# Column sums on TensorE in groups: the feature sums of ten layer norms in fours, the modulation sums in pairs

## The chip, the core and the metric

The kernel runs on one core of a Trainium2 chip. The metric is the device time of one execution in microseconds, lower is better. The core has five engines that work side by side, each through a queue of its own in order: TensorE (PE, matrix products; its weight loads are shown apart as PEld), VectorE (DVE), ScalarE (ACT), GpSimd (POOL) and SyncE (SP), which issues the DMA transfers here. They wait for each other through semaphores.

## The reference, cut to what matters

Two layers of a transformer over 1024 latent tokens and 256 context tokens, 1024 features wide. What the change touches is the layer norm and the modulation vectors:

```python
def layer_norm(x, g, b):
    mu = jnp.mean(xf, axis=-1, keepdims=True)
    var = jnp.mean(jnp.square(xf - mu), axis=-1, keepdims=True)
    return (xf - mu) * lax.rsqrt(var + LN_EPS) * g + b
...
for l in range(DEPTH):
    mod = silu_c @ w_ada[l] + b_ada[l]
    mod_c = silu_cc @ w_ada[l] + b_ada[l]
    sh1, sc1, g1, sh2, sc2, g2 = jnp.split(mod, 6, axis=-1)
    o, oc = token_mixers(modulate(x, sh1, sc1), modulate(xc, sh1c, sc1c), ...)
    x = layer_norm(ALPHA * x + g1 * (o @ w_out[l]), ln1_g[l], ln1_b[l])
    x = layer_norm(ALPHA * x + g2 * swiglu(modulate(x, sh2, sc2), ...), ln2_g[l], ln2_b[l])
```

In the first layer the context tokens take the same two residual steps and norms; in the last one they do not.

## The kernel before, in words

Everything is kept with the features on the partitions: a tensor of 1024 features is eight tiles of 128 partitions, with the tokens along the free axis (512, 512 and 256 of them). A dense product is done by `mm3` (L262): each f32 operand is split into a high and a low part (`wunit`, L234, does it for the weights: a DMA into `wraw`, an ACT cast `whi` on L249, a POOL or DVE subtraction `wlo` on L252), and three matmuls per feature tile, all on line L277, are summed in PSUM. `products_g` (L325) runs over the token groups, and an `evac` function takes each result out of PSUM. For the residual steps that is `ev_res` (L1172), which adds the gated product to the residual tile `z` with one DVE instruction (L1176).

A layer norm over features is a sum over partitions, and that is done by TensorE: `fsum` (L353) multiplies each of the eight feature tiles by a 128x32 block of ones. Tile `kt` goes to the column quarter `kt % 4` of the array, so to 32 of the 128 PSUM partitions, and the second four add to the first. The copy `fssb` (L360) takes the four partial sums out, and the next matmul (`mean` L377, or `var` L394) adds them over the quarters. `layer_norm` (L372) calls `fsum` twice: for `z` itself, and for the squares of `z` minus its mean, which ACT makes one by one into 512-wide buffers (`lnsq`, L388). Those buffers come from a pool of five (`t512`, L76) that the copies `fssb`, `meansb`, `rstdsb` and the modulation's `ut` share. After the variance come the reciprocal root on DVE (L343 to L349), `rstd` (L398), and the multiplication, the modulation and the affine step, feature tile by feature tile, on DVE, POOL and ACT. There are ten layer norms, eight over 512 tokens and two over 256. Each is put beside the dense products of the next token group; the last one, at the end of the kernel, has nothing beside it.

The modulation vectors of later stages are made in small steps between dense products. `ada_step` (L172) multiplies and adds one 128x512 block of `w_ada` into two accumulators on DVE (L177, L179), one for the latent and one for the context vector; after eight blocks each accumulator is summed over its partitions by one matmul against 32 columns of ones (L185, into `adaps`), on the quarter `2 * i + s_`. `ada_end` (L140) follows when both halves of a part are there. The first vectors (L138) are made in another way, which the change leaves alone.

The order of instructions in each engine's queue is made by a list scheduler, which simulates the times of the instructions and places each when it finds its inputs ready, earlier lines of the program first. The author steers it with edges: `gate(ins, after)` (L434) asks that `ins` is placed after `after`, with no semaphore, and `in_order` (L440) chains a list of instructions with such edges. `hook` (L297) ties the five steps of the 512-wide first layer norm of a layer to points in the dense matmuls that follow: the matmul that begins at column 6 x 512 of them is placed after the last sum of `z`, the one at 53 x 512 after the last sum of squares (L42).

Of the kernel before, what the change touches and what calls it, by code (L numbers as in the profile page):

```python
# [12 lines left out]
AF = mybir.ActivationFunctionType  # L13
ALU = mybir.AluOpType
# [8 lines left out]
KT = 8  # L23
# [30 lines left out]
def body(ctx: ExitStack, tc, xT, cT, w_ada, w_in, nbias, wa2, w_out, w_fi, w_fo, vecs, cc, consts, ropes, gmask, out):  # L54
    nc = tc.nc
    act, dve, pool, pe = nc.scalar, nc.vector, nc.gpsimd, nc.tensor
# [19 lines left out]
    def t512(name="t5"):  # L76
        return tmp.tile([P, 512], F32, tag="t5", name=name)
# [4 lines left out]
    def bank_x(name):  # L82
        return ps_x.tile([P, 512], F32, tag="x", name=name)

    def bank_a(name):
        return ps_a.tile([P, 512], F32, tag="a", name=name)
# [20 lines left out]
    ones = const.tile([P, 32], F32, name="ones")  # L107
# [10 lines left out]
    scc = const.tile([P, KT, 32], F32, name="scc")  # L118
# [21 lines left out]
    def ada_end(l, streams, ps, sel):  # L140
        sb = t512("adasb")
        act.copy(sb, ps)
        pv = bank_x("adav")
        for m in range(4):
            pe.matmul(pv[:, 4 * m:4 * m + 4], lhsT=sb[:, m * P:(m + 1) * P], rhs=sel, start=True, stop=True)
        for i, (part, half) in enumerate(streams):
            c0 = V_BADA + part * KT + half * 4
            dve.tensor_tensor(
                out=mod[l][:, part, half * 4:half * 4 + 4, :],
                in0=pv[:, 0:16].rearrange("p (m s) -> p m s", s=4)[:, :, 2 * i:2 * i + 2],  # L150
                in1=vec[l][:, c0:c0 + 4].unsqueeze(2).to_broadcast([P, 4, 2]), op=ALU.add)
# [13 lines left out]
    ada_todo, ada_run, ada_st = [], [], {}  # L165
# [6 lines left out]
    def ada_step(l, st, i, k, raw):  # L172
        if k == 0:
            ada_st["acc"] = [spool.tile([P, 512], F32, tag="hl", name="adacc") for _ in range(2)]
        for s_, a in enumerate(ada_st["acc"]):
            if k == 0:
                dve.tensor_scalar(a, raw, scc[:, k, s_:s_ + 1], None, ALU.mult)  # L177
            else:
                dve.scalar_tensor_tensor(out=a, in0=raw, scalar=scc[:, k, s_:s_ + 1], in1=a, op0=ALU.mult, op1=ALU.add)  # L179
        if k == KT - 1:  # L180
            if i == 0:
                ada_st["ps"] = bank_a("adaps")
            for s_, a in enumerate(ada_st["acc"]):
                q = 2 * i + s_
                pe.matmul(ada_st["ps"][32 * q:32 * q + 32, :], lhsT=ones[:, 0:32], rhs=a, start=True, stop=True)  # L185
            if i == 1:
                ada_end(l, st, ada_st["ps"], ident[:, 0:P:32])

# [108 lines left out]
    def hook(products_, offs):  # L297
        hk["c"] = 0
        hooks[:] = zip(offs, products_)
# [38 lines left out]
    def rsqrt_cols(src, n, eps, rows=P):  # L338
        v = small.tile([P, 20], F32, tag="rq_v", name="rq_v", bufs=2)
        y = small.tile([P, 20], F32, tag="rq_y", name="rq_y", bufs=2)  # L340
        t = small.tile([P, 20], F32, tag="rq_t", name="rq_t", bufs=2)
        v, y, t = v[:rows, :n], y[:rows, :n], t[:rows, :n]
        dve.tensor_scalar(v, src, eps, None, ALU.add)  # L343

        dve.tensor_scalar(y.bitcast(I32), v.bitcast(I32), -0.5, 1597463007.0, ALU.mult, ALU.add)
        for _ in range(3):
            dve.tensor_tensor(out=t, in0=y, in1=y, op=ALU.mult)
            dve.scalar_tensor_tensor(out=t, in0=t, scalar=-0.5, in1=v, op0=ALU.mult, op1=ALU.mult)
            dve.scalar_tensor_tensor(out=y, in0=t, scalar=1.5, in1=y, op0=ALU.add, op1=ALU.mult)  # L349
        return y  # L350


    def fsum(src, n):  # L353

        ps = bank_x("fs")
        for kt in range(KT):
            q = kt % 4
            ins = pe.matmul(ps[32 * q:32 * q + 32, :n], lhsT=ones[:, 0:32], rhs=src(kt), start=(kt < 4), stop=(kt >= 4))  # L358
        sb = t512("fssb")
        act.copy(sb[:, :n], ps[:, :n])  # L360
        return sb, ins
# [6 lines left out]

    NPOOL = 4
    NP3 = 3  # L370

    def layer_norm(z, t0, n, eps, consume, npool=NPOOL, offs=None):  # L372
        sl = slice(t0, t0 + n)
        nb = n // P
        sb, x1 = fsum(lambda kt: z[kt][:, sl], n)
        mps = bank_x("mean")
        x2 = pe.matmul(mps[:, :n], lhsT=onesm, rhs=sb[:, :n], start=True, stop=True)  # L377
        msb = t512("meansb")
        act.copy(msb[:, :n], mps[:, :n])
        for kt in range(KT):  # L380
            if kt >= KT - npool:
                pool.tensor_tensor(out=z[kt][:, sl], in0=z[kt][:, sl], in1=msb[:, :n], op=ALU.subtract)
            else:
                dve.tensor_tensor(out=z[kt][:, sl], in0=z[kt][:, sl], in1=mps[:, :n], op=ALU.subtract)

        def sq(kt):
            q = t512("lnsq")
            act.activation(q[:, :n], z[kt][:, sl], AF.Square)  # L388
            return q[:, :n]

        sb, x3 = fsum(sq, n)
        vps = bank_x("var")
        for b in range(nb):
            x4 = pe.matmul(vps[:, b:b + 1], lhsT=sb[:, b * P:(b + 1) * P], rhs=ones1, start=True, stop=True)  # L394
        y = rsqrt_cols(vps[:, :nb], nb, eps)
        rps = bank_x("rstd")
        for b in range(nb):
            x5 = pe.matmul(rps[:, b * P:(b + 1) * P], lhsT=y[:, b:b + 1].to_broadcast([P, P]), rhs=ident,  # L398
                           start=True, stop=True)
        if offs and n == 512:  # L400
            hook((x1, x2, x3, x4, x5), offs)
        rsb = t512("rstdsb")
        act.copy(rsb[:, :n], rps[:, :n])
        for kt in range(KT):
            if kt >= KT - npool:
                pool.tensor_tensor(out=z[kt][:, sl], in0=z[kt][:, sl], in1=rsb[:, :n], op=ALU.mult)
            else:
                dve.tensor_tensor(out=z[kt][:, sl], in0=z[kt][:, sl], in1=rps[:, :n], op=ALU.mult)
            consume(kt, sl)
# [24 lines left out]
    def gate(ins, after):  # L434

        if after is not None:
            tc.add_manual_dep(ins.ins, after.ins.name, NOSYNC, reason="buffers in order of use")
        return ins

    def in_order(inss):  # L440

        for a, b in zip(inss, inss[1:]):
            gate(b, a)
        return inss[-1]
# [80 lines left out]
    for l in range(NL):  # L525
# [35 lines left out]
        for e in range(2):  # L561
            ba = V[:, V_BA + e:V_BA + e + 1]
            for (t0, n) in FULL:
                ps = bank_q("zps")
# [4 lines left out]
        ins = [act.activation(a, a, AF.Exp, scale=-1.0) for a in dec][-1]  # L569
        ins = [gate(act.activation(a, a, AF.Ln, bias=one1), ins) for a in dec][-1]  # L570
# [24 lines left out]
        for p, ga, gb in abanks:  # L595
            dst, src, n = a_mm(p, ga, gb, gk, gq)
# [6 lines left out]
        for lev in range(6):  # L603
# [8 lines left out]
            for p, ga, gb in abanks:  # L612
                dst, src, n = a_mm(p, ga, gb, xk_, X)
# [87 lines left out]
        for p in range(2):  # L701
# [5 lines left out]
            for par in range(2):  # L707
                for g0, g1 in ((0, 8), (8, 10)):
                    pt = bank_q("inc")
                    for g in range(g0, g1):  # L710
                        for e in range(2):
                            for hh in range(2):
                                h, r0 = 2 * p + hh, 64 * e + 32 * hh
                                pe.matmul(pt[r0:r0 + 32, (g - g0) * 64:(g - g0 + 1) * 64],
                                          lhsT=kdt[e][64 * par:64 * par + 64, g * P + 32 * h:g * P + 32 * h + 32],
                                          rhs=vg(g)[64 * par:64 * par + 64, h * 64:(h + 1) * 64], start=True, stop=True)
# [13 lines left out]
            for i in range(1, NCH - 1):  # L730
                for e in range(2):
                    c, nx = order[e][i], order[e][i + 1]
# [3 lines left out]
                                             op0=ALU.mult, op1=ALU.add)  # L736
# [377 lines left out]
        sb = {"n": 0, "t": ps_s.tile([P, 2, 2, 512], F32, tag="s4", name="sT", bufs=1)}  # L1114
# [11 lines left out]
        for x, i in enumerate(PAIRS):  # L1126
            if x < 5:
                load(PAIRS[x + 1])
            if x in (0, 2):
# [3 lines left out]
            a, na, places, skip = (  # L1133
                (some(PAIRS[1], None), steps_a[3], 22, 2), (), (some(PAIRS[3], None), steps_a[3] - half, 22, 2), (),
                (some(PAIRS[5], None), steps_a[3] - half, 22, 2), (iter(()), 0, 39, 0))[x] or (
                chain(some(PAIRS[x + 2], half), some(PAIRS[x + 1], None)), half + steps_a[0], 39, 3)
            live, tails = tails, []
            b = stage_b(i)
            n = done = 0
# [22 lines left out]
        z = []  # L1162
# [9 lines left out]
        def ev_res(g, m):  # L1172
            def ev(ps, t0, n, c):
                s = 0 if t0 < SEQ else 1
                zz = z[m + c][:, t0:t0 + n]
                dve.scalar_tensor_tensor(out=zz, in0=ps[:, :n], scalar=g[:, m + c, s:s + 1], in1=zz,  # L1176
                                         op0=ALU.mult, op1=ALU.add)
            return ev

        groups = GROUPS[l]  # L1180
# [7 lines left out]
        for grp in groups:  # L1188
            for m in range(0 if grp[0][0] >= SEQ else 2, KT):
                dense(w_out[l, :, m * P:(m + 1) * P], oh_all, ol_all, grp, ev_res(ga1, m))  # L1190
            for (t0, n) in grp:
                def consume(kt, sl, t0=t0, n=n):
                    modulate(u2h, u2l, z[kt][:, sl], kt, l, 1, t0, n, dve)
                    affine(AFF1, z[kt][:, sl], aGB[:, 0, kt:kt + 1], aGB[:, 1, kt:kt + 1])
# [51 lines left out]
        for grp in GROUPS[l]:  # L1246
# [4 lines left out]
            for (t0, n) in grp:  # L1251
                def consume2(kt, sl, t0=t0, n=n):
# [6 lines left out]
                    elif t0 < SEQ:  # L1259
                        nc.sync.dma_start(xs[kt * P:(kt + 1) * P, sl], z[kt][:, sl])  # L1260
                layer_norm(z, t0, n, LN_EPS, consume2, NP3 if last else NPOOL)

# [99 lines left out]
```

## Time and profile before

| | us |
|---|---|
| median of three runs | 3704.74 (3701.15 to 3706.63) |
| the profiled execution | 3701.86 |
| its span in the profile | 3700.1 |
| mean granted clock of TensorE | 0.955 of full |

The profile is of one execution. Rows of groups read: line, engine, operation, out<-in, shape (rows*columns of the array that a matmul uses, then the size), x count, busy time in us, mean ns of one, idle time of the engine before them and who ended it. Rows of the timeline read: start in us from the span's start, length, engine, line, operation, count of merged records, and in brackets the idle time before with the one that ended it. Rows of the stretches view give a window, its length, the busy time of the engines, the granted clock, the share of the DMA engines in use and GB/s. An f32 matmul is run in two passes and leaves two records, so the 160 sum matmuls of the layer norms are 320 records on line 358:

```profile
L358 PE MATMUL fs<-z,ones x160: 379/592/636, 929.9 to 3673.1; 128*32 128x512 f32 x128, 128*32 128x256 f32 x32
L358 PE MATMUL fs<-lnsq,ones x160: 379/592/1062, 981.3 to 3683.0; 128*32 128x512 f32 x128, 128*32 128x256 f32 x32
```

A "visit" below is a run of consecutive matmuls of one such sum line in PE's order, between matmuls of other lines.

### The profile page before, as it was taken

To read this page: it belongs to the slowest core of one execution; us is meant where nothing else is said; L and a number is where in the kernel's file an instruction comes from. 1 tells how busy PE (TensorE), PEld (TensorE's weight loads), DVE (VectorE), ACT (ScalarE), POOL (GpSimd) and SP (SyncE) were. 2 spreads that over 40 slices of the span, in tenths; PEclk is the share of its full clock that TensorE was granted. 3 is DMA by queue.
4 is the path that set the end of the run, shared out by engine and by line. 5 is a ranking of instruction groups with operands and counts; after the bars stand their busy time and mean duration, and the time that the engine had idled before them with its cause. 6 is when DMAs were issued, how large, how long until landed. Compare 5 with 4: busy or idle time off the path is not lost.

```text
span 3700.1 us, 49312 instructions
## 1 busy us (share of the span) xinstructions
PE 3423.4 (93%) x20832; PEld 2536.6 (69%) x20832; DVE 1634.0 (44%) x2475; ACT 920.2 (25%) x1365; POOL 1243.6 (34%) x747
## 2 busy tenths in 40 slices
PE   6698997889999999999999969998889999999998
PEld 3587873434678888888876657783335688888875
DVE  3757555553444554454235553325552532222233
ACT  2213212333231111111114403212332311111113
POOL 1712304664451111111125552324663622222222
PEclk8799998999999999999999979998999999999998
DMA  5152240102221222221123212121103111111122
GB/s 174 42 159 78 96 178 20 63 1 79 70 60 63 90 84 74 75 94 61 35 74 95 72 58 72 60 106 46 58 1 103 49 43 56 47 47 52 47 72 85
DMA packets 287276, 262.93 MB, mean 71 GB/s; under 512 B 13840, under 2 KB 238416, under 8 KB 287056
## 3 DMA queue, kind: packets, MB, share of 16 engines
q1 hardware_dynamic: 287056, 259.80, 22.0%
q8 instruction: 163, 2.67, 0.3%
q14 instruction: 57, 0.47, 0.0%
HBM read 226.72 MB, written 33.03 MB: 70 GB/s over the span
## 4 chain that ended last, share of the span: by engine, by line
PE 81%; DVE 11%; ACT 4%; issue 2%; POOL 2%; DMA 1%; SPq 0%; ACTq 0%; DVEq 0%; POOLq 0%
PE mmps L277 60%; PE sT L476 4%; PE vps L656 3%; DVE m L935 3%; PE fs L358 2%; PE gav L951 2%; PE gs L484 2%; DVE S L735 1%; ACT gpt L1055 1%; DVE ut L229 1%; DVE slat L918 1%; PE nmT L459 1%; DVE ptl L1024 1%; PE spr L429 1%; PE adaps L185 1%
## 5 line engine op out<-in xcount | busy, mean ns | idle before, releaser
L252 POOL TENSOR_TENSOR wlo<-wraw,whi 128x1024 fp32r<-128x1024 f32 (+3 forms) x228 | 503.2, 2209 | 1770.5 <-ACT whi L249 1708.8
L277 PE MATMUL mmps<-oh,whi 128*128 128x512 f32 (+2 forms) x2416 | 905.8, 376 | 13.1 <-ACT whi L249 7.1
L277 PE MATMUL mmps<-oh,wlo 128*128 128x512 f32 (+1 forms) x2416 | 903.2, 374 | 2.6 <-POOL wlo L252 2.5
L277 PE MATMUL mmps<-ol,whi 128*128 128x512 f32 (+1 forms) x2416 | 902.5, 374 | 1.9 <-DVE ol L231 1.9
L277 PEld LDWEIGHTS mmps<-oh,whi 128*128 128x128 f32 (+1 forms) x2416 | 457.6, 189 | 122.5 <-issue 20.3
L277 PEld LDWEIGHTS mmps<-oh,wlo 128*128 128x128 f32 x2416 | 457.0, 189 | 114.5 <-issue 24.7
L277 PEld LDWEIGHTS mmps<-ol,whi 128*128 128x128 f32 x2416 | 457.5, 189 | 97.3 <-issue 16.6
L249 ACT CAST whi<-wraw 128x1024 fp32r<-128x1024 f32 (+3 forms) x262 | 251.8, 962 | 964.6 <-PE mmps L277 907.8
L1207 DVE TENSOR_TENSOR sg<-mmps,sg 128x512 f32<-128x512 f32 (+1 forms) x110 | 70.1, 637 | 603.0 <-PE mmps L277 598.7
L277 PE MATMUL mmps<-hl,whi 128*128 128x512 f32 (+1 forms) x880 | 324.8, 370 | 1.0 <-DVE hl L1209 1.0
L277 PE MATMUL mmps<-hh,whi 128*128 128x512 f32 (+1 forms) x880 | 324.1, 371 | 0.0
L277 PE MATMUL mmps<-hh,wlo 128*128 128x512 f32 (+1 forms) x880 | 321.2, 369 | 0.0
L1176 DVE SCALAR_TENSOR_TENSOR z<-mmps,mod,z 128x512 f32<-128x512 f32 (+1 forms) x320 | 217.8, 694 | 198.4 <-PE mmps L277 197.6
L179 DVE SCALAR_TENSOR_TENSOR adacc<-adaw,scc,adacc 128x512 f32<-128x512 f32 x280 | 239.2, 897 | 92.8 <-DMA adaw<-in_w_ada_dram 92.3
L1047 POOL TENSOR_TENSOR gacc<-gacc,gpt 128x1024 f32<-128x1024 f32 x80 | 189.9, 2375 | 80.7 <-ACT gpt L1055 80.5
L935 DVE TENSOR_REDUCE m<-gs 128x2 f32<-128x1024 f32 (+1 forms) x150 | 154.8, 1032 | 107.6 <-PE gs L484 107.6
L277 PEld LDWEIGHTS mmps<-hh,whi 128*128 128x128 f32 x880 | 165.9, 189 | 41.3 <-issue 9.2
L277 PEld LDWEIGHTS mmps<-hh,wlo 128*128 128x128 f32 x880 | 165.6, 189 | 31.9 <-issue 2.5
L277 PEld LDWEIGHTS mmps<-hl,whi 128*128 128x128 f32 x880 | 166.2, 189 | 30.1 <-DVE hl L1209 1.2
L277 PE MATMUL mmps<-uh,whi 128*128 128x512 f32 (+3 forms) x408 | 155.6, 388 | 28.4 <-ACT uh L230 18.8
L1055 ACT ACTIVATE gpt<-sT 128x1024 f32<-128x1024 f32 x120 | 122.9, 1024 | 182.2 <-PE sT L476 166.9
L1209 DVE TENSOR_TENSOR hl<-sg,hh 128x512 fp32r<-128x512 f32 (+1 forms) x110 | 128.7, 1170 | 67.1 <-ACT hh L1208 67.1
(238 smaller groups left out, 4636.7 us busy)
## 6 DMA issues: line engine op xcount, KB each, us to landing
wraw<-in_w_fi_dram SPq DMA_DIRECT2D x106, 512.0 KB, 3.9
adaw<-in_w_ada_dram SPq DMA_DIRECT2D x160, 256.0 KB, 3.6
wraw<-in_w_fo_dram SPq DMA_DIRECT2D x60, 384.0 KB, 3.1
wraw<-in_w_in_dram SPq DMA_DIRECT2D x40, 512.0 KB, 3.9
wraw<-in_w_out_dram SPq DMA_DIRECT2D x36, 512.0 KB, 3.6
sp<-sphi SPq DMA_DIRECT2D x40, 256.0 KB, 2.0
sp<-splo SPq DMA_DIRECT2D x40, 256.0 KB, 2.1
adaw<-in_w_ada_dram SPq DMA_DIRECT2D x16, 512.0 KB, 7.3
```

The lines of the kernel that those rows point to most:

```text
L179: dve.scalar_tensor_tensor(out=a, in0=raw, scalar=scc[:, k, s_:s_ + 1], in1=a, op0=ALU.mult, op1=ALU.add)
L249: act.copy(a[:, :m], rw)
L252: (dve if pace["lo"] and pace["w"] % pace["lo"] == 0 else pool).tensor_tensor(out=b[:, :m], in0=rw, in1=f(a[:, :m]), op=ALU.subtract)
L277: ins = pe.matmul(o, lhsT=lhs, rhs=rhs, start=st, stop=(k == nk - 1 and lhs is b))
L358: ins = pe.matmul(ps[32 * q:32 * q + 32, :n], lhsT=ones[:, 0:32], rhs=src(kt), start=(kt < 4), stop=(kt >= 4))
L476: inss = [pe.matmul(ps[:, e, :n], lhsT=w[rows(e), c0:c0 + P], rhs=m[rows(e), q0:q0 + n], start=(i == 0), stop=(i == 3)) for i, (w, m, c0) ...
L656: ins = pe.matmul(ps[:, :256], lhsT=lhs, rhs=rhs, start=(k == 0 and i == 0), stop=(k == KT - 1 and i == 2))
L935: dve.tensor_reduce(out=m3[:, j, :, c], in_=ps[:, :, :n], axis=AX.X, op=ALU.max)
L1047: (dve if q and i == 5 else pool).tensor_tensor(out=acc[q], in0=prev if kb == 1 else acc[q], in1=pt, op=ALU.add)
L1055: act.activation(pt, ps, AF.Exp)
L1176: dve.scalar_tensor_tensor(out=zz, in0=ps[:, :n], scalar=g[:, m + c, s:s + 1], in1=zz, op0=ALU.mult, op1=ALU.add)
L1209: dve.tensor_tensor(out=b_[:, sl], in0=sg[:, sl], in1=f(a_[:, sl]), op=ALU.subtract)
```

## The change

In `fsum` the eight matmuls are issued as two groups of four, one on each column quarter. The four inputs of a group are asked for first. The four matmuls are chained in order, and the first is placed after the instruction that makes the fourth input: the square of that tile, or for sums of `z` the residual step of that tile and token group, which `ev_res` now notes in `z_last`. In `ada_step` the two matmuls of a half are chained, and the first is placed after the last DVE accumulation. All these edges are placing edges without a semaphore; what is computed, and the number of instructions on each engine, stay as they are.

```diff
@@ ada_step
         for s_, a in enumerate(ada_st["acc"]):
             if k == 0:
-                dve.tensor_scalar(a, raw, scc[:, k, s_:s_ + 1], None, ALU.mult)
+                ins = dve.tensor_scalar(a, raw, scc[:, k, s_:s_ + 1], None, ALU.mult)
             else:
-                dve.scalar_tensor_tensor(out=a, in0=raw, scalar=scc[:, k, s_:s_ + 1], in1=a, op0=ALU.mult, op1=ALU.add)
+                ins = dve.scalar_tensor_tensor(out=a, in0=raw, scalar=scc[:, k, s_:s_ + 1], in1=a, op0=ALU.mult,
+                                               op1=ALU.add)
...
-            for s_, a in enumerate(ada_st["acc"]):
-                q = 2 * i + s_
-                pe.matmul(ada_st["ps"][32 * q:32 * q + 32, :], lhsT=ones[:, 0:32], rhs=a, start=True, stop=True)
+            inss = [pe.matmul(ada_st["ps"][32 * q:32 * q + 32, :], lhsT=ones[:, 0:32], rhs=a, start=True, stop=True)
+                    for q, a in enumerate(ada_st["acc"], 2 * i)]
+            gate(inss[0], ins)
+            in_order(inss)
@@ fsum
-        for kt in range(KT):
-            q = kt % 4
-            ins = pe.matmul(ps[32 * q:32 * q + 32, :n], lhsT=ones[:, 0:32], rhs=src(kt), start=(kt < 4), stop=(kt >= 4))
+        for k0 in (0, 4):
+            rhs, made = zip(*(src(k0 + q) for q in range(4)))
+            inss = [pe.matmul(ps[32 * q:32 * q + 32, :n], lhsT=ones[:, 0:32], rhs=rhs[q], start=(k0 == 0), stop=(k0 == 4))
+                    for q in range(4)]
+
+            gate(inss[0], made[3])
+            ins = in_order(inss)
@@ layer_norm
-        sb, x1 = fsum(lambda kt: z[kt][:, sl], n)
+        sb, x1 = fsum(lambda kt: (z[kt][:, sl], z_last.get((kt, t0))), n)
...
-            act.activation(q[:, :n], z[kt][:, sl], AF.Square)
-            return q[:, :n]
+            return q[:, :n], act.activation(q[:, :n], z[kt][:, sl], AF.Square)
@@ ev_res
-                dve.scalar_tensor_tensor(out=zz, in0=ps[:, :n], scalar=g[:, m + c, s:s + 1], in1=zz,
-                                         op0=ALU.mult, op1=ALU.add)
+                z_last[m + c, t0] = dve.scalar_tensor_tensor(out=zz, in0=ps[:, :n], scalar=g[:, m + c, s:s + 1],
+                                                             in1=zz, op0=ALU.mult, op1=ALU.add)
```

More of the change, by code (lines that the diff above doesn't have):

```diff
@@ L370, in body @@
     NP3 = 3
+    z_last = {}
     def layer_norm(z, t0, n, eps, consume, npool=NPOOL, offs=None):
```

## The prediction

> **What bounds the kernel now.** I read the page's totals and its chain of work that ended last, then the stretches that hold the layer norms.
>
> ```profile
> span 3700.1 us, 49312 instructions
> PE 3423.4 (93%) x20832; PEld 2536.6 (69%) x20832; DVE 1634.0 (44%) x2475; ACT 920.2 (25%) x1365; POOL 1243.6 (34%) x747
> ...
> PE 81%; DVE 11%; ACT 4%; issue 2%; POOL 2%; DMA 1%; SPq 0%; ACTq 0%; DVEq 0%; POOLq 0%
> ```
>
> ```profile
> 971.00:1026.00 55.00, 50.57 (x202) 32.67 (x202) 28.69 (x43) 18.09 (x26) 32.19 (x21) 0.94 0.21 57
> 1943.00:2010.00 67.00, 66.92 (x274) 43.78 (x274) 37.89 (x53) 25.64 (x38) 38.31 (x23) 1.00 0.30 95
> 2877.00:2925.00 48.00, 46.18 (x195) 29.92 (x194) 27.51 (x43) 18.11 (x26) 32.26 (x21) 1.00 0.19 56
> ```
>
> Each row of the second fence is a stretch: its length, then busy PE, PEld, DVE, ACT, POOL, then the granted clock, the DMA share and GB/s. PE is busy for 92 to 99.9% of them, the next engine, POOL, for at most two thirds (32.26 of 48). So where the feature sums lie beside dense matmuls, a microsecond of PE is a microsecond of the kernel. The last layer norm, after 3662, is the exception: nothing dense is left there.
>
> What a sum costs is read in the timeline (start, length, what, count of records; one f32 matmul leaves two records).
>
> ```profile
> 941.57 0.39 PE L277 MATMUL mmps<-ol,whi 128*128 128x512 f32 x1
> 941.80 0.39 PE L277 MATMUL mmps<-oh,wlo 128*128 128x512 f32 x1
> 942.12 1.04 PE L358 MATMUL fs<-z,ones 128*32 128x512 f32 x2
> 943.09 0.50 PE L277 MATMUL mmps<-oh,whi 128*128 128x512 f32 x1
> ...
> 2893.30 0.39 PE L277 MATMUL mmps<-oh,whi 128*128 128x512 f32 x1
> 2893.62 1.06 PE L358 MATMUL fs<-lnsq,ones 128*32 128x512 f32 x8
> 2894.61 0.50 PE L277 MATMUL mmps<-ol,whi 128*128 128x512 f32 x1
> ```
>
> Dense matmuls start 0.23 us apart. With one sum matmul between them, 941.80 to 943.09 is 1.29 us: the visit costs 1.29 - 0.23 = **1.06 us**. With four sum matmuls on the four column quarters, 2893.30 to 2894.61 is 1.31 us, so 1.08. The price is that of a visit to the 128x32 form; the second to fourth matmul in it add 0.02 together.
>
> **The change part by part.** *Feature sums, 512 wide.* How many visits there are today follows from the busy time of line 358 (stretches view, that line alone: length, busy PE and records), since a visit is 1.05 us of it.
>
> ```profile
> 929.00:972.00 43.00, 7.24 (x16) 1.00 0.30 86
> ...
> 3628.00:3642.00 14.00, 5.25 (x16) 1.00 0.22 66
> sum 281.00, PE 81.61; mean PE 5.83
> ```
>
> These are the first, the last and the sum of the fourteen 512-wide feature sums beside dense work: 81.61 / 1.05 = 78 visits. In fours they are 14 x 2 = 28. So 50 visits go, 50 x 1.06 = **53.0 us**, and none of the 320 sum records. The two sums of the last layer norm are outside this count and come below.
>
> *Feature sums, 256 wide* (context tokens, four of them):
>
> ```profile
> 2043.99 0.28 PE L277 MATMUL mmps<-hl,whi 128*128 128x256 f32 x1
> 2044.20 0.62 PE L358 MATMUL fs<-z,ones 128*32 128x256 f32 x2
> 2044.75 0.38 PE L277 MATMUL mmps<-hh,whi 128*128 128x256 f32 x1
> ...
> sum 49.00, PE 12.02; mean PE 3.00
> ...
> 2048.10 0.73 PE L358 MATMUL fs<-z,ones 128*32 128x256 f32 x2 [2.30 <-DVE z L1176]
> ```
>
> A visit here is 2044.75 - 2043.99 - 0.12 = 0.64 us. The busy sum of 12.02 us holds a few full-width gaps; counted in the listing there are 16 visits, of which 8 stay: 8 x 0.64 = 5.1 us at most. But the sums of z lie next to waits for other engines (here 2.30 us for an eviction), where a freed PE only waits longer. From 0 to 5.1; I take 3.0, the visits that have no wait beside them and half of the rest.
>
> *Modulation sums.* Each is a pair of matmuls on two quarters.
>
> ```profile
> L185 PE MATMUL adaps<-adacc,ones 128*32 128x512 f32 x80 | 25.9, 605 | 1.8 <-DVE adacc L179 1.8
> ```
>
> 25.9 / 1.05 is 24.7; the listing shows 24 visits for 20 pairs, one of them 0.66 us longer. Four go: 4 x 1.06 = **4.2 us**. The last accumulation on DVE that the pair is held for is needed by its second matmul anyway.
>
> *What the hold adds.* An order edge is no instruction; nothing is added to any queue, no DMA moves. But PE works its queue in order: if the order was drawn up with a fourth input that comes later on the chip, all the dense matmuls behind the group wait, and behind them DVE and ACT, which evict them, and the weight buffers. Today the sums' own waits are these, in the four tables of PE's waits (us in total, times, longest):
>
> ```profile
> PE fs L358 <- DVE z L1176: 0.7, 1, 0.7
> ...
> PE fs L358 <- DVE z L1176: 2.3, 1, 2.3
> PE fs L358 <- ACT lnsq L388: 1.4, 2, 1.1
> ```
>
> 4.4 us in all beside dense work. Per group the new wait lies between 0 and the longest, 2.3; I take 0.1 for each of 40 groups, **4 us**, nearest to what today's visits waited.
>
> The hold also keeps buffers. The squares share five 512-wide buffers with the mean's copy. Now square five needs the mean's copy to be free or a sum to have run, as the tail shows:
>
> ```profile
> 3676.20 3.74 POOL L382 TENSOR_TENSOR z<-z,meansb 128x512 f32<-128x512 f32 x3 [10.14 <-ACT meansb L379]
> 3676.88 5.18 ACT L388 ACTIVATE lnsq<-z 128x512 f32<-128x512 f32 x8 [0.75 <-DVE z L384]
> 3677.56 6.25 PE L358 MATMUL fs<-lnsq,ones 128*32 128x512 f32 x16 [2.06 <-ACT lnsq L388]
> 3683.85 0.59 ACT L360 COPY fssb<-fs 128x512 f32<-128x512 f32 x1 [1.79 <-PE fs L358]
> ```
>
> There eight squares run through in 5.18 us (0.65 each). With four held, the fourth is done at 3679.5, the fifth starts when POOL lets go of the mean at 3679.94, the sixth when the first group has run (1.3 us after 3679.5, so 3680.8), the eighth ends near 3682.8 and the copy starts near 3684.6 in place of 3683.85: **0.8 us** more, bare on the end of the kernel (0 to 2). Inside dense work the same delay is covered by the matmuls, and there the squares are paced by PE today:
>
> ```profile
> 982.38 0.63 ACT L388 ACTIVATE lnsq<-z 128x512 f32<-128x512 f32 x1 [1.21 <-PE fs L358]
> ...
> 1015.37 0.58 PE L277 MATMUL mmps<-oh,whi 128*128 128x256 f32 x1 [4.43 <-ACT whi L249]
> ```
>
> With fewer visits that chain gets shorter too. What doesn't follow PE is the wait at 1010 to 1015: a weight cast sits in ACT's queue behind casts of the modulation. Four square visits (4.2 us) lie between the sum that starts that layer norm and this wait; if its DVE and ACT work ends no earlier, they come back as waiting. I take 4 us off for this one place (0 to 4.2).
>
> *A rule against it.* Eight records in a visit take 0.02 us more than two. The Trainium skill, "TensorE: Matmul & The Clock Gate", section "The cost: per-tile semaphore tail", says that increments of a semaphore by packed matmuls serialize, and gives 25 + 4.7 per tile + 26.3 per increment in ns. By it, an estimate, a visit of four that each release a buffer would be 0.09 us longer than a visit of one, and the gain 3 us smaller; the trace shows only the 0.02.
>
> **Sum.** 53.0 + 3.0 + 4.2 - 4.0 - 0.8 - 4.0 = 51.4 us off. The profiled execution took 3701.9 us (span 3700.1 and 1.8 around it), so 3650.5; the median of the runs shown is 2.9 above it, and most executions lie between. I say **3652 us**.
>
> **The rivals.** *Groups fall apart.* The edges order the four but don't forbid dense matmuls between them; if the hold is met when the fourth input's instruction is merely queued, the group comes as three and one. Against it speak the sums of the softmax, an order chain of four already:
>
> ```profile
> L491 PE MATMUL sums<-acc,ones 128*32 128x512 f32 x48 | 6.4, 602 | 2.1 <-ACT NM L462 2.1
> ```
>
> 48 records are six chains of four; 6.4 us is 1.07 each, one visit's time: none of them is broken. Broken once everywhere, 56 of the 78 visits stay and only 22 x 1.06 = 23 us are saved; less 4.8 for waits and tail, 18 us: 3686.
>
> *The saving comes back as waits.*
>
> ```profile
> sum 91.00, PE 38.67; mean PE 5.53
> ```
>
> This is line 358 over the seven sums of squares beside dense work (972 to 991 the first, 3628 to 3642 the last): by the listing 36 of the 78 visits, so 36 - 14 = 22 of the 50 that go lie behind the start of their layer norm. If the chain mean, subtraction, square, rstd, modulation on DVE, ACT and POOL then ends last in all of them, 23 us are lost instead of 4: 3671. For: the wait of 4.43. Against: POOL at two thirds, and squares that wait for PE.
>
> *Slower.* One mechanism: the held groups stand at the head of PE's queue and wait for the fourth input, each as long as the longest wait of today, 2.30 us. 40 x 2.3 = 92 us against 60 gained, so about 3705 + 32 = 3737. It turns from gain to loss at 60 / 40 = 1.5 us per group. Against: only one of today's sums beside dense work waits over 1.5 us.
>
> *No change*: the order comes out as before, 3704; the visits' count would have to stay at 97.
>
> **How the numbers follow.** Forecast 0.66 (own range 3640 to 3670), waits 0.14, broken groups 0.12, no change 0.04, slower 0.04. The low end is the sum with all bounds in its favour, 53.0 + 5.1 + 4.2 = 62 us off, 3642, and a little for a shorter layer norm chain: 3637. The high end takes in both weaker gains: 3688. A measurement of this kernel tells about 0.2%, 7 us, from no change: faster 0.92, same 0.04, slower 0.04.
>
> **What would show it.** Right: line 358's records come as x8, some 40 visits in all, and its busy time beside dense work falls from 81.61 + 12.02 = 93.6 us to some 35 (28 x 1.06 and 8 x 0.64); line 185 shows twenty visits; dense matmul time is unchanged. Broken groups: x6 and x2 apart, some 70 visits. Waits: few visits, but PE idle behind lnsq, whi or ut that grows by tens of microseconds. Tail: the copy of the last sum of squares 0.8 us later behind the mean than now. The forecast is wrong if the price belongs to the matmuls after all, so that a visit of four beside dense work takes well over 1.1 us, or if the new order moves work in stages that the change doesn't touch.

## The result, and the profile after

The changed kernel takes **3677.48 us** (median), the kernel before on the same chip 3704.28: a ratio of **0.9922 [0.9908, 0.9936]**, 27 us less. A second series gave 3673.78 against 3701.87, 0.9927 [0.9914, 0.9939]. One of the first series' four executions took 6558.48 us, for a reason that isn't known; it is counted in the median (3676.97 without it) and not in the ratio. The forecast was 3652, so 52 us less: the sign is right, the size is half.

The page of the changed kernel, its totals and the last line of the chain of waits:

```profile
span 3666.8 us, 49303 instructions
PE 3388.7 (92%) x20832; PEld 2528.3 (69%) x20832; DVE 1639.5 (45%) x2475; ACT 918.8 (25%) x1365; POOL 1244.2 (34%) x747
...
PE 81%; DVE 11%; ACT 3%; issue 2%; POOL 2%; DMA 1%; SPq 0%; ACTq 0%; DVEq 0%; POOLq 0%
```

PE is busy 34.7 us less and is still what bounds the kernel. This execution took 3668.58 us; why that is 9 us under the median comes below. The sums by shape, first in the groups of the kernel before, then after:

```profile
L358 PE MATMUL fs<-z,ones 128*32 128x512 f32 x128 | 47.9, 605 | 0.1
L358 PE MATMUL fs<-lnsq,ones 128*32 128x512 f32 x128 | 44.9, 660 | 3.5 <-ACT lnsq L388 3.5
```

```profile
L360 PE MATMUL fs<-lnsq,ones 128*32 128x512 f32 x128 | 37.2, 632 | 2.3 <-ACT lnsq L395 2.3
L360 PE MATMUL fs<-z,ones 128*32 128x512 f32 x128 | 32.1, 632 | 1.4 <-DVE z L1182 1.4
L184 PE MATMUL adaps<-adacc,ones 128*32 128x512 f32 x80 | 25.9, 605 | 1.6 <-DVE adacc L179 1.6
```

The busy time of the 512-wide sums fell from 92.8 to 69.3 us; the part of it beside dense work fell from 81.6 to 58.9 us (below), where the forecast wanted 28 x 1.06 = 29.7. The modulation sums (25.9 us) didn't move at all. The stretches that hold the fourteen 512-wide sums beside dense work, line 360 alone (length, busy PE and records, clock, DMA share, GB/s), the first, the last and the sum:

```profile
929.00:967.90 38.90, 2.83 (x16) 1.00 0.33 95
...
3596.00:3608.00 12.00, 5.25 (x16) 1.00 0.25 76
sum 236.00, PE 58.86; mean PE 4.20
```

A whole sum in two visits would be 2.1 us; the last one here has 5.25, five visits. The timeline of PE shows why, at the sum of `z` in the first layer's second norm:

```profile
1909.73 1.05 PE L360 MATMUL fs<-z,ones 128*32 128x512 f32 x2
1910.70 0.50 PE L279 MATMUL mmps<-hh,whi 128*128 128x512 f32 x1
1911.04 0.40 PE L279 MATMUL mmps<-hl,whi 128*128 128x512 f32 x1
1911.37 1.05 PE L360 MATMUL fs<-z,ones 128*32 128x512 f32 x2
...
3571.75 1.06 PE L360 MATMUL fs<-z,ones 128*32 128x512 f32 x6
...
3573.87 1.04 PE L360 MATMUL fs<-z,ones 128*32 128x512 f32 x2
```

Here the four of a group are four visits with two dense matmuls between each and the next; at 3571 another group is three and one. The groups' inner order holds, and so does the place of the first behind the instruction that makes the fourth input, but nothing keeps dense matmuls out. Counting runs of consecutive sum matmuls in PE's order:

| visits | before | after | sums of `z` alone grouped | squares alone grouped | with a waiting edge | and `z` in eights |
|---|---|---|---|---|---|---|
| 512 wide, z + squares | 42 + 36 | 25 + 30 | 25 + 36 | 42 + 28 | 17 + 13 | 7 + 13 |
| 256 wide, z + squares | 10 + 6 | 6 + 5 | 9 + 6 | 7 + 5 | 4 + 4 | 2 + 4 |
| modulation | 24 | 24 | 24 | 24 | 20 | 20 |

(The last layer norm's visits are left out: three in each kernel, two with `z` in eights. The totals in the text count them in: 97 before, 69 after, 41 with a waiting edge, 28 with eights.) The change removes 23 visits of 512 and 5 of 256, where the forecast removed 50 and 8, and 4 of modulation.

### The profile page after: what moved, and what is told of

It is laid out like the page before. It is cut to its first block, busy times and chain, and to the rows that moved or that the text cites. A ratio compares the mean times of both kernels' runs of the same rounds, so it can differ in the third digit from the quotient of the medians.

```text
span 3666.8 us, 49303 instructions
## 1 busy us (share of the span) xinstructions
PE 3388.7 (92%) x20832; PEld 2528.3 (69%) x20832; DVE 1639.5 (45%) x2475; ACT 918.8 (25%) x1365; POOL 1244.2 (34%) x747
## 4 chain that ended last, share of the span: by engine, by line
PE 81%; DVE 11%; ACT 3%; issue 2%; POOL 2%; DMA 1%; SPq 0%; ACTq 0%; DVEq 0%; POOLq 0%
PE mmps L279 60%; PE sT L482 4%; PE vps L662 3%; DVE m L941 3%; PE gav L957 2%; PE fs L360 2%; PE gs L490 2%; DVE S L741 1%; ACT gpt L1061 1%; DVE slat L924 1%; DVE ut L231 1%; PE nmT L465 1%; PE spr L435 1%; DVE ptl L1030 1%; PE adaps L184 1%
## 5 line engine op out<-in xcount | busy, mean ns | idle before, releaser
L279 PE MATMUL mmps<-oh,wlo 128*128 128x512 f32 (+2 forms) x2416 | 901.5, 374 | 5.1 <-POOL wlo L254 3.7
L279 PE MATMUL mmps<-ol,whi 128*128 128x512 f32 (+2 forms) x2416 | 901.1, 373 | 4.9 <-DVE ol L233 4.9
L279 PEld LDWEIGHTS mmps<-oh,wlo 128*128 128x128 f32 (+1 forms) x2416 | 456.4, 189 | 108.3 <-issue 18.4
L279 PEld LDWEIGHTS mmps<-ol,whi 128*128 128x128 f32 (+1 forms) x2416 | 456.7, 189 | 99.7 <-issue 15.6
```

Of the source, the lines that this page charges most:

```text
L279: ins = pe.matmul(o, lhsT=lhs, rhs=rhs, start=st, stop=(k == nk - 1 and lhs is b))
```

## The experiments

**The same kernel again.**

> The changed kernel once more. Theory (visits): its order has 69 visits to the 128x32 form for the layer norms where the kernel before has 97, 23 fewer of 512 columns and 5 fewer of 256, and 24 as before for the modulation sums: 23 x 1.06 + 5 x 0.64 = 27.6 us less, about 3677. Rival (the profiled execution's 33 us is the true gain, and some 6 us come from the order of other work): about 3670. Either way the profile shows whether the 8.5 us that the first profile won in the middle of the second layer (2291 to 2379, with no feature sum in it) come again.

3673.78 us, midway between theory and rival, 0.9927 [0.9914, 0.9939]; the profiled span is 3672.0 us. Comparing the starts of the same PE matmuls stage by stage, it agrees with the first profile within 0.4 us everywhere but ahead of 921 us, before the first layer norm: there this execution is 5.3 us behind the profile of before and the first one 0.3 ahead of it. This part differs between executions of one order, so a single profile of this kernel is good to some 5 us, and the stages are compared one by one below.

**The order edge made into a wait** (groups with a waiting edge).

```diff
-            gate(inss[0], ins)              # ada_step
+            hold(inss[0], ins)
-            gate(inss[0], made[3])          # fsum
+            hold(inss[0], made[3])
+    def hold(ins, after):
+        if after is not None:
+            tc.add_manual_dep(ins.ins, after.ins.name, SYNC, reason="a group comes when its last input is there")
```

`SYNC` is the class of edge that asks for the end of the other instruction, where `gate` asks for its place only.

> The edge from the fourth input becomes one with a wait for its end, so the four come together: 55 visits outside the last layer norm become 30 of 512 columns (78 in the kernel before) and 8 of 256 (16 before), and 20 for the modulation sums (24 before). Theory (the gain is the number of visits): 48 x 1.06 + 8 x 0.64 + 4 x 1.06 = 60 us, less 0.8 for the tail, so about 3645. Rival (freed PE time comes back as waits for squares and casts): half of what is gained beyond the changed kernel is lost, about 3661. Rival (the hold itself stalls PE's queue): 3680 or more, with PE idle behind lnsq and z.

> The kernel with the waiting edge once more, to stand on the same chip beside the next ones: 0.9881 of the kernel before, some 44 us less, in the first measurement. Theory (visits at 1.19 us, less waits that come back): the same, 0.987 to 0.990.

3657.84 us, **0.9881 [0.9868, 0.9895]**, and in the second series 3660.26, 0.9876 [0.9858, 0.9893]. The groups of this kernel:

```profile
L185 PE MATMUL adaps<-adacc,ones 128*32 128x512 f32 x80 | 21.0, 605 | 3.1 <-DVE adacc L180 3.1
L361 PE MATMUL fs<-z,ones 128*32 128x512 f32 x128 | 20.6, 616 | 2.1 <-DVE z L1188 2.1
L361 PE MATMUL fs<-lnsq,ones 128*32 128x512 f32 x128 | 18.8, 662 | 11.3 <-ACT lnsq L396 11.3
```

And its timeline:

```profile
1915.55 1.07 PE L361 MATMUL fs<-z,ones 128*32 128x512 f32 x8
```

Now the groups come as the forecast saw them: 41 visits of feature sums against 69, twenty of modulation. 28 visits of feature sums fewer than in the change, but only some 16 us less, nearer to the rival's 3661 than to 3645. The rest is lost to waits and to a lower granted clock of TensorE, taken up below: from the end of the first attention on PE idles 151.3 us here and 138.1 in the change's second profile, and the clock's mean over the run is 0.950 here and 0.955 there.

**One kind of sum at a time.** In `fsum` the edges are set only `if grouped:`, for `z` or for the squares; those of `ada_step` are off.

> The change's edges on the sums of z alone; squares and modulation sums as before. Its order has 17 fewer visits of 512 columns and 1 fewer of 256 than the kernel before. Theory (visits): 17 x 1.06 + 0.6 = 18.7 us, about 3686. Rival (the gain belongs to the squares, whose buffers PE paced): about 3700.

> The change's edges on the sums of squares alone; sums of z and modulation sums as before. Its order has 8 fewer visits of 512 columns and 4 fewer of 256 than the kernel before. Theory (visits): 8 x 1.06 + 4 x 0.64 = 11.0 us, about 3693. Rival (the gain belongs to the squares): 25 us, about 3679.

`z` alone 0.9965 [0.9951, 0.9978], 11.8 us; squares alone 0.9975 [0.9966, 0.9984], 9.8 us. From the visits 18.7 and 11.0 were expected. Together 21.6 us, and the change gives 27 to 28.

**No edges at all**: the changed code, which builds the four inputs ahead of the four matmuls, without any order edge.

> The changed source without its placing edges: the instructions of the kernel before in the same order. It gives a second profile of that order. Theory (the first attention stage, 565 to 615, and the start of the second layer's linear attention, 2291 to 2374, differ by several us between executions of one order): its profile lies up to 5 us off the first one there. Rival (the 8 us that the changed kernel wins at 2291 to 2374 come from its order): there it is within 1 us of the first profile, with the wait of 6 us for ms.

3703.91 us, 1.0002 [0.9991, 1.0012]. So the gain belongs to the edges and not to the rewritten loops.

**The price of a visit.** In the kernel before, in the middle (k = 4) of 68 products of the second layer's hidden units, an f32 matmul into an unused bank is added, kept between two dense ones by order edges. What it computes isn't used.

```diff
+            if k == 4 and n == 512 and pace.get("probe"):
+                probe, pd = ins, bank_x("probe")
+                for q in range(1):
+                    probe = gate(pe.matmul(pd[32 * q:32 * q + 32, :n], lhsT=ones[:, 0:32], rhs=f(pick(xh[k])), start=True, stop=True), probe)
```

The second kernel has `range(4)`, one on each column quarter; the third has `pd[:, :n], lhsT=ident`, one over the whole array.

> The kernel before with 68 matmuls of 32 columns added, each alone between two dense matmuls of the second layer's hidden products; their results are not used. It prices a visit by itself. Theory (the price is the visit's, 1.06 us): 68 x 1.06 = 72 us more, about 3776. Rival (beside steady dense work it is only the matmul's own two passes, 0.46): 31 us more, about 3735.

> As the kernel with 68 single matmuls added, but with four in each place, one on each column quarter. Theory (three more in a visit cost 0.02 together): 68 x 1.08 = 73 us more than the kernel before, about 3777. Rival (the price is the matmul's): four times the single one's, 270 us or more above the kernel before.

> As the kernel with 68 single matmuls added, but each uses all 128 columns, as the dense ones beside it do. Theory (most of a visit's price is the way into the 128x32 form and back): only the two passes, 68 x 0.46 = 31 us more than the kernel before, about 3735. Rival (an f32 matmul costs that much in any form): 72 us more, about 3776.

| added at 68 places | us | ratio | us per place |
|---|---|---|---|
| one on a quarter | 3784.87 | 1.0223 [1.0209, 1.0238] | 80.9 / 68 = 1.19 |
| four, one on each quarter | 3787.20 | 1.0227 [1.0212, 1.0241] | 83.2 / 68 = 1.22 |
| one over the whole array | 3764.23 | 1.0167 [1.0153, 1.0182] | 60.2 / 68 = 0.89 |

PE's timeline with one on a quarter:

```profile
3030.78 0.39 PE L282 MATMUL mmps<-oh,wlo 128*128 128x512 f32 x1
3031.10 1.04 PE L278 MATMUL probe<-oh,ones 128*32 128x512 f32 x2
3032.08 0.50 PE L282 MATMUL mmps<-oh,whi 128*128 128x512 f32 x1
3032.41 0.39 PE L282 MATMUL mmps<-ol,whi 128*128 128x512 f32 x1
```

With one over the whole array:

```profile
3023.10 0.39 PE L282 MATMUL mmps<-oh,wlo 128*128 128x512 f32 x1
3023.33 1.02 PE L278 MATMUL probe<-oh,cst 128*128 128x512 f32 x2
3023.78 0.80 PE L282 MATMUL mmps<-oh,whi 128*128 128x512 f32 x1
3024.42 0.40 PE L282 MATMUL mmps<-ol,whi 128*128 128x512 f32 x1
```

Two things are to be seen. From 3030.78 to 3032.41 are 1.63 us for two dense steps of 0.23 and the visit: 1.17. The forecast stopped at the first dense matmul behind the visit; that one starts late, and its follower comes 0.33 behind it instead of 0.23, which is part of the price too. And the whole-array matmul costs 0.89 by itself (here 1.32 - 0.46 = 0.86), so three quarters of a visit's price are the f32 matmul and only 1.19 - 0.89 = 0.3 us the change of form; neither the 31 us expected for the third kernel nor its rival's 72 came. The matmul's two records, called two passes further up, cost nearly four dense steps. The price is that of the visit all the same: three more matmuls on the other quarters add 0.03.

For 256 columns there is no such run. In the profile before, the follower of the visit at 2044.20 starts at 2044.97, so 2043.99 to 2044.97 are 0.98 us for two dense steps of 0.12 and the visit: 0.74, where the forecast read 0.64. The sums below go by 0.64; with 0.74 each such visit is worth 0.1 us more.

The Trainium skill, "FP8 and Floating Point Precision", section "TensorE Precision Notes", says that true FP32 takes 4 passes through the array. By it, an estimate, the f32 matmul costs four dense steps, 4 x 0.23 = 0.92 us; the 0.89 agrees.

**Fewer visits still**: as with the waiting edge, but the eight matmuls of a sum of `z` as one group, held for the eighth input.

> As the kernel with the waiting edge, but the eight matmuls of a sum of z come in one visit, held for the eighth input; the sums of squares stay in fours. Theory (visits): 7 visits of eight matmuls, 1.06 + 0.46 us each, 13 of four, and 2 + 4 of 256 columns: 512 wide 82.7 - 24.4 = 58.3 us less than before, 256 wide 5.9, modulation 4.2, tail some 1.4 more: 67 us, about 3637. Rival (waits): the mean starts half a microsecond later in each layer norm and nothing further is gained, about 3645 to 3655.

28 visits of feature sums instead of 41, and 3663.28 us, 0.9893 [0.988, 0.9907]: not faster, and its interval overlaps that of groups of four. PE's waits for `z` at these sums grow from 2.6 to 8.2 us in all, and at the start of the second layer stands a wait of 7.3 us for the scale of a norm that the groups of four don't have. The eights are also worth less than their number says: a visit of eight is not one visit's price. From the dense matmul at 2842.76 to the second one behind the visit, at 2845.27, are 2.51 us for two dense steps and the visit, so 2.05 against 1.22 for four, and the seven eights in place of seventeen visits save 17 x 1.22 - 7 x 2.05 = 6 us. The wait of 7.3 isn't the eights' own doing: the kernels with one kind of sum grouped have it too (below). Stage by stage this profile is 7 to 8 us ahead of the two of groups of four outside 2233 to 2811 (times of the kernel before, from 921 on) and 7 us behind them in it; what eights would give without that wait stays open.

**One norm left ungrouped.** With the waiting edge, the second norm of the first layer has its sums as before from token 512 on, which puts 9 visits of 512 and 6 of 256 back.

```diff
+        held = not (eps == LN_EPS and npool == NPOOL and t0 >= 512)
-            hold(inss[0], made[3])
+            if held:
+                hold(inss[0], made[3])
```

> As the kernel with the waiting edge, but the second layer norm of the first layer is left ungrouped for tokens 512 to 1023 and for the context: 9 more visits of 512 columns and 6 more of 256. Theory (there the weight units and the modulation end last, so a freed PE only waits): as long as with them grouped, within 4 us. Rival (a visit costs its 1.19 us, the 256-wide one 0.72, wherever it is): 9 x 1.19 + 6 x 0.72 = 15 us longer than with them grouped.

These visits are 9 x 1.19 + 6 x 0.64 = 14.6 us of PE. The kernel takes 3663.09 us, 0.9886 [0.9868, 0.9903], 2.8 us more than with them grouped in the same series; the intervals overlap, and the theory's 4 us hold. Most of what grouping takes off in that norm comes back there. PE's waits in it with all groups held (1965 to 2060; us in total, times, longest):

```profile
PE mmps L280 <- ACT oh L233: 3.0, 1, 3.0
PE mmps L280 <- DVE wlo L255: 2.7, 1, 2.7
PE mmps L280 <- POOL wlo L255: 2.1, 3, 0.9
PE mmps L280 <- DVE ol L234: 2.0, 1, 2.0
PE mmps L280 <- ACT whi L252: 1.4, 1, 1.4
PE fs L361 <- DVE z L1188: 0.9, 2, 0.5
PE fs L361 <- ACT lnsq L396: 0.8, 1, 0.8
```

And with this norm left ungrouped (1965 to 2070):

```profile
PE fs L361 <- DVE z L1191: 2.3, 1, 2.3
PE fs L361 <- ACT lnsq L399: 1.4, 2, 1.1
PE mmps L280 <- DVE hl L1224: 1.0, 1, 1.0
PE mean L388 <- ACT fssb L369: 0.5, 1, 0.5
```

5.2 us of waits became 12.9 (and 0.3 in one more row), and what is late is mainly not the sums but the dense matmuls' own operands: the halves of the next input and of the weights, which ACT, DVE and POOL make. Ungrouped visits had covered them.

Waits are not all of it. Two stretches between the same two matmuls, from ahead of that norm to the dense work behind it (length, then busy PE, PEld, DVE, ACT, POOL, then the clock), first grouped, in its second series, then ungrouped:

```profile
1907.30:2210.30 303.00, 255.11 (x2027) 197.05 (x2026) 161.86 (x206) 89.78 (x138) 162.12 (x105) 0.87 0.26 81
1908.40:2214.30 305.90, 261.78 (x2027) 195.38 (x2026) 158.79 (x206) 89.51 (x138) 162.10 (x105) 0.89 0.26 80
```

With the same 2027 records grouping saves 2.9 us. PE idles 3.8 us more (47.9 against 44.1) and is busy only 6.7 us less, not 14.6: its granted clock is 0.87 instead of 0.89, which on 303 us is some 6 us, an estimate.

**One more buffer for the squares**: the waiting edge, and the pool of the squares with six buffers instead of five.

> As the kernel with the waiting edge, with six 512-wide buffers in the pool that the squares use, in place of five. Theory (four held squares and the mean's copy fill the five, so the sixth square waits for the first group): of PE's 11.3 us of waiting for squares most goes, in the last layer norm some 2 us of bare time, in all 4 to 9 us less than with five. Rival (the squares wait for the subtractions): no difference over 2 us.

3665.15 us, 0.9892 [0.9877, 0.9908], against 0.9876 without: no gain, where 4 to 9 us were expected. The waits that it aims at do get shorter: over the whole run PE waits 11.3 us for squares with five buffers (seven times), and with six:

```profile
PE fs L361 <- ACT lnsq L396: 8.3, 6, 3.9
PE msq L427 <- DVE ms L428: 6.4, 1, 6.4
```

But a wait of 6.4 us for the scale of a norm has come in, in an order that came out otherwise. The buffers are a part of the waits (3 us), and no better kernel comes of it.

## Where the time went, stage by stage

The table compares the start of one and the same PE matmul at each stage's ends. "Visits" is what the feature-sum visits removed are worth at 1.19 and 0.64 us; negative is time lost. Each column is one profile.

| stage, times of the kernel before | after | visits | with a waiting edge | visits |
|---|---|---|---|---|
| to the end of the first attention, 0 to 921 | +0.3, -5.3 again | 0 | -5.7 | 0 |
| first layer, first norms, 921 to 1248 | 13.3 | 12.5 | 13.8 | 16.8 |
| first layer, second norms, 1815 to 2101 | 2.7 | 7.3 | 9.9 | 25.3 |
| second layer to the end of its attention, 2101 to 2811 | 8.5 | 0 | 6.1 | 0 |
| second layer, first norms, 2811 to 3149 | 4.0 | 7.1 | 6.4 | 11.9 |
| second layer, second norm, 3401 to 3671 | 3.6 | 3.6 | 8.3 | 8.3 |
| last norm, 3671 to the end | 0.8 | | -2.2 | |

Three things stand in it.

The stages with sums give 23.6 us for 30.5 us of visits, with the waiting edge 38.4 for 62.3. In the last of them, 3401 to 3671, the price holds to the tenth: PE alone bounds there. In the first layer's second norms most of it is lost, to waits as just shown and to the clock: between the matmuls at 1920 and 2101 PE idles 5.3 us before and 13.7 with the waiting edge, at a granted clock of 0.99 and 0.96.

8.5 us of the change's gain come in a stage with no feature sum. In the kernel before, at the start of the second layer, PE waits once for the scale of a norm (2280 to 2380):

```profile
PE mmps L277 <- DVE ms L421: 6.0, 1, 6.0
```

The kernel without edges has this wait at the same place, 4.4 us, and takes the same time as the kernel before from 2291 to 2374, within 0.5 us: what the change gains there comes from its order, not from another execution. The changed one has in its place 1.6 and 0.5 us (2268 to 2362):

```profile
PE rot L767 <- DVE ms L427: 1.6, 1, 1.6
PE ops L814 <- DVE ms L427: 0.5, 1, 0.5
```

The stretches there, in the kernel before (length, then busy PE, PEld, DVE, ACT, POOL, then the clock):

```profile
2291.40:2329.80 38.40, 32.42 (x209) 27.00 (x198) 29.05 (x81) 10.54 (x25) 5.00 (x3) 0.87 0.05 15
2329.80:2374.10 44.30, 44.30 (x343) 35.68 (x341) 15.79 (x41) 10.60 (x17) 14.92 (x10) 0.92 0.24 78
```

and in the changed kernel between the same matmuls, in its second series:

```profile
2280.80:2314.40 33.60, 31.54 (x206) 26.12 (x198) 28.94 (x80) 10.19 (x24) 5.07 (x3) 0.94 0.06 17
2314.40:2355.50 41.10, 41.10 (x343) 33.48 (x341) 16.11 (x41) 10.60 (x17) 14.95 (x10) 1.00 0.26 84
```

4.8 us go in the first stretch, with less waiting, and 3.2 in the second, where PE is busy throughout with the same 343 matmuls at a clock of 1.00 instead of 0.92. Both profiles of the changed kernel show it. The clock doesn't go with this wait: with the waiting edge the wait is as short (0.9 and 0.5 us), and the second stretch runs at 0.92 again, in 43.9 us. The kernels with only `z` or only the squares grouped have a wait of 8.1 and 7.5 us for this scale again, in the same stage, which fits the 6 us that their gains together fall short of the whole. It is a new order of work that the edges led to, not fewer visits. Which edge tips it, and why the clock is higher in the changed kernel, stays open.

The first 921 us differ by up to 6 us between profiles: without edges -2.6, in the others +0.3 to -5.7 against this profile of before. Between the two of the changed kernel, which are of one order, PE's busy time there grows from 780.6 to 788.3 us, at a granted clock of 0.91 and 0.90. That the first profiled execution lies 9 us under the median fits this, for the larger part; of the executions without a profile no stages are known.

## Why the prediction was off

The time lies within the range of 3637 to 3688, though outside the forecast's own 3640 to 3670, and not by the way that was forecast. That it came out 9 us under the 3686 of "groups fall apart" is luck, a gain of 8.5 us that no term names.

**"In fours they are 14 x 2 = 28" failed.** It took the fourth input's place in the order for a hold on the group. The edge asks that the first matmul stand behind that instruction in the order and not that its result be there. 23 of the 50 visits went, and the rival "groups fall apart" (3686, given 0.12) is what happened, only not everywhere: the count of 69 is the "some 70" named there. The forecast took the softmax's whole chains of four as evidence against it; those are a pure order chain too, but stand among other work, and say nothing of how the sums are placed. Why the planner puts dense matmuls between is argued, not shown: with the edge to the place alone, the first of the group is free while the other inputs aren't yet there, and dense work that is ready goes first. The run with the waiting edge shows that this edge decides it.

**"The visit costs 1.06"** was right in kind and low in size: 1.19, because the second dense matmul behind it is late as well. The profile before had this already: the matmul behind 943.09 starts at 943.43. That four in a visit cost about what one does (0.02 more forecast) held, 0.03. No tail of 0.09 for matmuls that each release a buffer was seen: four squares in a visit take 1.65 us to the second dense start behind them (2893.30 to 2894.95 before), four `z`, which release none there, take 1.65 too (1915.23 to 1916.88 with the waiting edge).

**Modulation, 4.2 us**: nothing. Its last accumulation is indeed needed by the second matmul, but the first was not kept back for it; with the waiting edge the four visits go (25.9 to 21.0 us of busy time).

**256 wide, 3.0 us**: five visits went, 5 x 0.64 = 3.2, so the size came out by luck: five visits at full price (3.7 us at 0.74) instead of eight at part.

**Waits of the held groups, 4 us**: the change holds no group back, so it has none (2.3 for squares against 3.5 before). With a true hold the sums' own waits for squares are 11.3 us, of which 5.7 stand in the last norm.

**4 us for the wait at 1010 to 1015**: with groups whole, that stage gives 13.8 for 16.8 us of visits, so 3.0 lost. The size fits, the place doesn't: that one wait is 4.43 us before and 4.45 with the waiting edge, while PE's waits for `whi` in the stage grow from 7.1 us (two) to 9.6 (four) and 2.0 for squares come in. What the forecast left out is loss elsewhere: 15.4 us in the first layer's second norms, part of it by the lower clock, and 5.5 in the second layer's first. So "the saving comes back as waits" (3671) is in good part the right picture for whole groups; that the stretches were 92 to 99.9% busy on PE said only that PE was late there by then, not by how much the next engine was early.

**Tail, 0.8 us more.** From the mean's copy to the copy of the last sum of squares were 8.31 us before, with the waiting edge 9.61, so 1.30 more; the change itself has 7.76:

```profile
3643.05 0.59 ACT L386 COPY meansb<-mean 128x512 f32<-128x512 f32 x1 [1.21 <-PE mean L384]
...
3650.81 0.59 ACT L366 COPY fssb<-fs 128x512 f32<-128x512 f32 x1 [1.14 <-PE fs L360]
```

With the waiting edge it goes as the forecast described, four squares, one, three:

```profile
3635.79 0.59 ACT L387 COPY meansb<-mean 128x512 f32<-128x512 f32 x1 [1.21 <-PE mean L385]
3637.13 2.48 ACT L396 ACTIVATE lnsq<-z 128x512 f32<-128x512 f32 x4 [0.75 <-DVE z L392]
3640.23 0.63 ACT L396 ACTIVATE lnsq<-z 128x512 f32<-128x512 f32 x1 [0.61 <-POOL z L390]
3641.62 1.67 ACT L396 ACTIVATE lnsq<-z 128x512 f32<-128x512 f32 x3 [0.76 <-PE fs L361]
3645.40 0.59 ACT L367 COPY fssb<-fs 128x512 f32<-128x512 f32 x1 [2.11 <-PE fs L361]
```

**Work moved in stages that the change doesn't touch** was named as what would make the forecast wrong and put into no term: +8.5 us. In sum, the change's 28 us of its second series are 24.2 in the stages with sums, 8.4 of the new order in the second layer, 0.8 at the end, and -5.3 in the first 921 us; the 27 of the first series are medians of executions that differ in that first part.

## What to carry to other kernels

An edge that orders places does not keep a group together; where matmuls are to come in one piece on the array, tie the first to the end of the last input, and count the visits in PE's order before pricing them. Here that version is the better one: 0.9881 and 0.9876 against 0.9922 and 0.9927. Price what is removed stage by stage and hold against it how early the operands of the next dense matmuls are: a full PE hides by how little the others are ahead. Read the granted clock beside the waits: here both took from the gain.

## What the chip showed that was not expected

An f32 matmul of 512 columns costs 0.89 us over the whole array, nearly four dense steps of 0.23, so a single sum matmul on 32 columns (1.19) is dear above all for its type, and the change of form adds just 0.3 us.

The same matmuls, with PE busy throughout, took 41.1 us at a granted clock of 1.00 and 44.3 at 0.92. The wait ahead of them doesn't tell which: with the waiting edge it is short, and they run at 0.92. Over the whole run the kernel with a waiting edge, where PE idles more, has the lower mean clock, 0.950 and 0.949 in its two profiles against 0.957 and 0.955 in the change's. The cause of neither is shown.

Eight of these f32 matmuls in one visit, two on each quarter, cost 2.05 us, four 1.22.
